# The scale and the sign of a softmax moved upstream, and two weight loads asked for earlier

## The chip, the cores and the metric

One core of a Trainium2 chip runs the whole program. The metric is the time of one execution on the device in microseconds (us); lower is better. The program before was timed three times; the median is compared. Engines are named as the profile does: PE is TensorE's matrix multiplication (PEld its weight loads, which overlap it), DVE is VectorE, ACT is ScalarE, POOL is GpSimd, SP is SyncE, which here only issues transfers.

## What is computed

Two layers of a decoder over 16 learned tokens and 1024 tokens, model width 1024. Layer 0 mixes with a recurrence and pooling, layer 1 with causal differential attention; after each mixer stand an output projection and an MLP. The change touches the attention of layer 1 and the beginning of what follows it. Of the reference:

```python
def one_block(args):
    qblk, start = args
    s = jnp.einsum('bqhcd,bkhcd->bhcqk', qblk, k).astype(jnp.float32) * scale
    qpos = start + jnp.arange(Q_BLOCK)
    mask = kpos[None, :] <= qpos[:, None]
    s = jnp.where(mask, s, -jnp.inf)
    p = jax.nn.softmax(s, axis=-1)
    attn = p[:, :, 0] - lam * p[:, :, 1]
    return jnp.einsum('bhqk,bkhe->bqhe', attn.astype(v.dtype), v)
...
for i in range(DEPTH):
    ...
    h = h + rmsnorm(m, g[1])
    f = sq_relu_mlp(rmsnorm(h, g[2]), mlp_w1[i], mlp_w2[i])
    h = h + rmsnorm(f, g[3])
```

Here q and k have 8 heads with two components c of 64 channels each, and scale is 1/8.

## The kernel before

All matrices are float32. A product of two of them is done as three products of halves: each operand is split into a rounded part "hi" (a copy on ACT) and the rest "lo" (a subtraction on DVE or POOL).

**The attention (mixer1)** goes over 8 heads, and in a head over 8 blocks of 128 queries (attn_block). The queries of a component are split in `halves` (L1756 on ACT, L1757 on DVE) into one operand qst that holds hi and lo; each key operand stands as kh and kl. In a block, for each component c, PE writes the scores s to a PSUM tile (L1824, L1826, and L1828 for the causal mask); there are two such tiles. DVE takes the row maximum into a column of m: where the block has up to 512 keys, one reduce for both components (L1834), above that one for each (L1831). The last block of a head has 1040 keys; the last 16 of both components stand in a tile se of their own and are folded in by L1836 and L1838. Then L1839 multiplies both columns of m by -1/8, and ACT forms exp(s/8 + m) with the row sum (L1843; L1845 for the 16 keys). L1850 and L1851 invert the sums, L1855 (ACT) and L1856 (DVE) combine the two components. The result is transposed on PE (L1870), split (L1873 on ACT, L1874 on DVE) and multiplied with the values (L1896 to L1903).

Beside this, work of the next head stands in the program: its weights are loaded to the one buffer R[0] with two halves (L360), split (L361 on ACT, L362 on POOL) and used in projections psq and psv (L377 to L379). In the last head, 7, there is no next head. There the first part of the output projection stands instead (`early`): loads of the earlier heads' outputs ho (L1533), their split (L397, L398), products pse (L377 to L379), a copy pz (L527) and its store to the DRAM tensor part (L528).

The order of mixer1 is not the text's. The framework schedules the instructions with its own estimates of their durations, so that an edit in one place can move rows on all engines. Each engine and each transfer queue then takes its row strictly in order.

**The late region (late)** ends the layer: the rest of the output projection (`tiles`), norms, and the MLP. For layer 1 it first needs five pieces of the output weights in split form: two narrow ones wl (128x640), which hold the last two row blocks for the five column blocks that `early` has begun, and three wide ones wo (128x1024). They are loaded to buffers raw (L669; R[0] takes the first two and the last, a second buffer the two between) and split into tiles opb (L670 on ACT, L671 on DVE). A product of `tiles` (L691) is 6 matmuls with wl or 24 with wo. What part holds is loaded to ac (L673, one load for each half of the tokens) and added (L721). The order here is set by the class Flow, a planner with costs of its own. The buffers of the late region lie where those of mixer1 were, and an instruction that first writes such a place waits for the last reader of what was there.

Of the kernel before, what the change touches and what calls it, by code (L numbers as in the profile page):

```python
# [7 lines left out]
F32 = mybir.dt.float32  # L8
F32R = mybir.dt.float32r
AF = mybir.ActivationFunctionType  # L10
ALU = mybir.AluOpType
# [4 lines left out]
T = 1040  # L16
NM = 16
# [46 lines left out]
LW = ((768, 768, 1024, 1024), (640, 640, 1024, 1024, 1024))  # L64
# [257 lines left out]
class Trunk:  # L322
# [231 lines left out]
    def late(self, l, xs, part, hin, hmid, hout, pre, rsb):  # L554

        nc, tc, A = self.nc, self.tc, self.A
# [32 lines left out]
        S = [rp.tile([P, NH], F32, name=f"ss{i}") for i in (0, 1)]  # L589
# [73 lines left out]
        for i in range(len(n)):  # L663
            hi, lo = self.lw(i)
            if True:
                z = ("R", i % 4 // 2, i % 2)
                raw = R[i % 4 // 2][:, i % 2, :n[i]]
                if l or i > 1:
                    F.dma(lambda raw=raw, i=i: nc.sync.dma_start(raw, self.lw_src(l, i)), n[i] * 512, w=[z])  # L669
                F.act(n[i], lambda raw=raw, hi=hi: nc.scalar.copy(hi, raw), r=[z], w=[("L", i, 0)])  # L670
                F.dve(n[i], lambda raw=raw, hi=hi, lo=lo: tt(lo, raw, hi.bitcast(F32), op=ALU.subtract), r=[z, ("L", i, 0)], w=[("L", i, 1)])  # L671
            if i < 2:
                F.dma(lambda h=i: nc.sync.dma_start(m[h][:, :ne], self.rows(part, off + NH * h, NH)), ne * P * 4 * NH, w=sum((nM(i, k) for k in range(ne)), []))  # L673
# [244 lines left out]
        for j in range(14):  # L918
# [7 lines left out]
            c = {11: 0, 21: 1, 22: 2, 12: 7}  # L926
# [49 lines left out]
        for b in range(4):  # L976
            nk = 4 if b < 3 else 2
            for q, i in enumerate(order):
                p = place[was[q]]
                st, z = H3[q % 2], nH(q % 2)  # L980
# [45 lines left out]
        for x in (0, 1):  # L1026
            st, z = H3[x], nH(x)
# [609 lines left out]
    def mixer1(self, hn):  # L1637
        tc, nc, A, dr = self.tc, self.nc, self.A, self.dr
        self.o1d = dr.tile([8, P, 1024], F32, name="o1d")
        part = dr.tile([5 * P, T], F32, name="part1")  # L1640
        lam_init = 0.8 - 0.6 * math.exp(-0.3)
        with tc.tile_pool(name="dps", bufs=2, space=PSUM, reuse_waits="tile") as dps, \
             tc.tile_pool(name="sps", bufs=2, space=PSUM, reuse_waits="tile") as sps, \
             tc.tile_pool(name="tps", bufs=1, space=PSUM, reuse_waits="tile") as tps, \
             tc.tile_pool(name="aps", bufs=1, space=PSUM, reuse_waits="tile") as aps, \
             tc.tile_pool(name="ep", bufs=1, reuse_waits="tile") as ep:
            self.dps, self.sps, self.tps, self.aps, self.ep = dps, sps, tps, aps, ep
            self.tp = ep
            self.cs = ep.tile([P, 2, T], F32, name="cs")
            nc.sync.dma_start(self.cs, A["rope"])  # L1650
            lv = ep.tile([P, 4, C], F32, name="lv")
            nc.sync.dma_start(lv, A["lamv"])
            self.identb = ep.tile([P, P], mybir.dt.bfloat16, name="identb")
            nc.vector.tensor_copy(self.identb, self.con[:, K_ID:K_ID + P])
            self.maskb = ep.tile([P, P], mybir.dt.bfloat16, name="maskb")
            cau = ep.tile([P, 512], F32, tag="sb", name="cau", bufs=4)[:, :P]
            nc.sync.dma_start(cau, A["con"][:, K_CAU:K_CAU + P])
            nc.vector.tensor_copy(self.maskb, cau)
            nc.vector.tensor_tensor(lv[:, 0:2], lv[:, 0::2], lv[:, 1::2], op=ALU.mult)
            l2 = ep.tile([P, 2], F32, name="l2")  # L1660
            nc.vector.tensor_reduce(l2, lv[:, 0:2], axis=mybir.AxisListType.X, op=ALU.add)
            nc.scalar.activation(l2, l2, AF.Exp)
            self.nlam = ep.tile([P, 1], F32, name="nlam")
            nc.vector.scalar_tensor_tensor(self.nlam, l2[:, 1:2], -lam_init, l2[:, 0:1], op0=ALU.add, op1=ALU.subtract)
            self.sub = ep.tile([P, 1], F32, name="sub")
            nc.vector.tensor_scalar(self.sub, self.par[:, C_SUB:C_SUB + 1], (lam_init - 1.0) * 0.5 / P, None, op0=ALU.mult)
            self.pt, self.ov = {}, {}
            wide = [w.rearrange("p a b -> p (a b)") for w in self.WP]
            self.ring, self.turn = [(wide[0], wide[1]), (wide[2], ep.tile([P, 1024], F32R, name="wpx"))], 0
            self.given = [((wide[0], wide[1]),), (None,)]  # L1670
            self.quarters = QS[1]
            xs = [[] for _ in QS[1]]
            early = self.early(xs, A["wo_1"], part, 6, 5)
            load = lambda k: [0 for _ in self.loads(xs, self.o1d, (k,), NM, 2)]
            fill = [lambda k=k: load(k) for k in range(6)] + [lambda: next(early)] * (4 * 5)
            fill.insert(max(len(fill) - 9, 6), lambda: load(6))
            qkv, first = self.attn_in(0, hn)
            for i in [0, 5, 1, 6, 10, 11, 2, 7, 3, 4, 12, 8, 9, 13, 14, 15]:
                first[i]()
            for b in (0, 1):  # L1680
                self.pt[0, b] = self.attn_block(0, b, qkv)
            for h in range(8):
                nxt, side = self.attn_in(h + 1, hn) if h < 7 else (None, fill[:30])
                main = self.attn(h, qkv, nxt)
                at = (0, 6, 12, 12, 14, 15, 16, 24, 24, 24, 24, 24, 24, 24, 29, 29) if h < 7 else [0 + i * 2 for i in range(len(side))]
                i = 0
                for n, f in enumerate(main):
                    while i < len(side) and at[i] <= n:
                        side[i]()
                        i += 1  # L1690
                    f()
                for f in side[i:]:
                    f()
                qkv = nxt
            for f in fill[30:]:
                f()
            for c in range(4):
                xs[c].append(self.x7[c])
            self.late_x = xs
        return part  # L1700

    def attn_in(self, h, hn):
        nc, ep, cs = self.nc, self.ep, self.cs
# [47 lines left out]
        def halves(nme):  # L1751
            for c in (0, 1):
                d = tl[nme, c]
                if nme == "q":
                    st = ep.tile([P, 1024], F32R, tag="qst", name=self.nm("qst"), bufs=2)
                    nc.scalar.copy(st, d[:, :1024])  # L1756
                    nc.vector.tensor_tensor(st[64:128], d[64:128, :1024], st[64:128].bitcast(F32), op=ALU.subtract)  # L1757
                    res["q", c] = st
                else:
                    kh = ep.tile([P, T], F32R, tag="kh", name=self.nm("kh"), bufs=2)  # L1760
                    kl = ep.tile([P, T], F32R, tag="kl", name=self.nm("kl"), bufs=2)
                    nc.scalar.copy(kh, d)
                    for a, b, e in ((0, 640, nc.vector), (640, T, nc.gpsimd)):
                        e.tensor_tensor(kl[:, a:b], d[:, a:b], kh[:, a:b].bitcast(F32), op=ALU.subtract)
                    res["k", c] = (kh, kl)
# [36 lines left out]
    def attn_block(self, h, i, qkv):  # L1802
        nc, ep = self.nc, self.ep
# [6 lines left out]
        for c in (0, 1):  # L1810
# [17 lines left out]
                    nc.tensor.matmul(out(x0, x1), self.identb, self.maskb[:, x0 - m0:x1 - m0], start=False, stop=True)  # L1828
            S.append(sp)
            if L > 512:  # L1830
                nc.vector.tensor_reduce(m2[:, c:c + 1], sp[:, :L0], axis=mybir.AxisListType.X, op=ALU.max)  # L1831
        if L <= 512:
            s3 = S[0].rearrange("p (c k) -> p c k", c=2)[:, :, :L]
            nc.vector.tensor_reduce(m2[:, 0:2], s3, axis=mybir.AxisListType.X, op=ALU.max)  # L1834
        if se is not None:
            nc.vector.tensor_reduce(m2[:, 4:6], se[:, :2 * NM].rearrange("p (c k) -> p c k", c=2),  # L1836
                                    axis=mybir.AxisListType.X, op=ALU.max)
            nc.vector.tensor_tensor(m2[:, 0:2], m2[:, 0:2], m2[:, 4:6], op=ALU.max)  # L1838
        nc.vector.tensor_scalar(m2[:, 0:2], m2[:, 0:2], -0.125, None, op0=ALU.mult)  # L1839
        pr = []  # L1840
        for c in (0, 1):
            p = ep.tile([P, T], F32, tag=f"p{c}", name=self.nm("p"), bufs=1 if c else 3)
            nc.scalar.activation(p[:, :L0], S[c][:, :L0], AF.Exp, bias=m2[:, c:c + 1], scale=0.125, accum_out=m2[:, 2 + c:3 + c])  # L1843
            if se is not None:
                nc.scalar.activation(p[:, 1024:T], se[:, c * NM:(c + 1) * NM], AF.Exp, bias=m2[:, c:c + 1], scale=0.125,  # L1845
                                     accum_out=m2[:, 6 + c:7 + c])
            pr.append(p)
        if se is not None:
# [236 lines left out]
```

## Time and profile before

| | us |
|---|---|
| median of 3 runs | 2778.07 (2774.0 to 2783.71) |
| the profiled execution | 2771.01 |
| its span, first to last instruction | 2769.1 |
| PE busy | 2614.2 (94%) |
| DVE busy | 2032.5 (73%) |
| ACT busy | 1342.7 (48%) |
| POOL busy | 290.4 (10%) |
| mean granted TensorE clock | 0.974 |

The attention of layer 1 lies about between 1440 and 2024 us of the span, the late region of layer 1 from there to the end. A row of the timeline has the start in us, the duration, the engine and the line, what is written<-read, and in brackets how long the engine stood idle before it and whom it waited for. A row with xN merges N neighbours. A row of the waits view has the waiting engine and line, the one waited for, then total us, times, and the longest. The row of a line has its duration in ns as smallest/median/largest.

### The profile page before, as it was taken

To read this page: it belongs to the slowest core of one execution; us is meant where nothing else is said; L and a number is where in the kernel's file an instruction comes from. 1 tells how busy PE (TensorE), PEld (TensorE's weight loads), DVE (VectorE), ACT (ScalarE), POOL (GpSimd) and SP (SyncE) were. 2 spreads that over 40 slices of the span, in tenths; PEclk is the share of its full clock that TensorE was granted. 3 is DMA by queue.
4 is the path that set the end of the run, shared out by engine and by line. 5 is a ranking of instruction groups with operands and counts; after the bars stand their busy time and mean duration, and the time that the engine had idled before them with its cause. 6 is when DMAs were issued, how large, how long until landed. Compare 5 with 4: busy or idle time off the path is not lost.

```text
span 2769.1 us, 44824 instructions
## 1 busy us (share of the span) xinstructions
PE 2614.2 (94%) x16950; PEld 2381.9 (86%) x16950; DVE 2032.5 (73%) x3742; ACT 1342.7 (48%) x2779; POOL 290.4 (10%) x410
## 2 busy tenths in 40 slices
PE   7999998899999999999968999999889999999997
PEld 6899897899899999999956899898787788778877
DVE  5356876534977777888786887888648778778888
ACT  5456776544633334343344556555636333443342
POOL 0111334220000000000012222222000000000000
PEclk9999998899999999999988999999999999999998
DMA  4456777554324345443332222222243243543443
GB/s 152 172 183 187 244 220 222 179 162 150 142 101 170 137 164 193 169 153 132 107 112 73 59 77 68 62 67 62 77 159 137 103 167 150 194 172 137 152 160 122
DMA packets 198575, 391.27 MB, mean 141 GB/s; under 512 B 59984, under 2 KB 122328, under 8 KB 185944
## 3 DMA queue, kind: packets, MB, share of 16 engines
q1 hardware_dynamic: 171176, 348.24, 37.8%
q10 hardware_dynamic: 27184, 40.18, 4.0%
q8 instruction: 133, 2.18, 0.3%
q14 instruction: 82, 0.67, 0.1%
HBM read 240.06 MB, written 131.38 MB: 134 GB/s over the span
## 4 chain that ended last, share of the span: by engine, by line
PE 64%; DVE 10%; ACT 4%; issue 2%; DMA 2%; POOL 0%; DVEq 0%; SPq 0%; ACTq 0%; POOLq 0%
PE bank L691 44%; PE psq L377 2%; PE psq L378 2%; PE psq L379 2%; PE ps L292 1%; PE s L1824 1%; PE tr L1870 1%; PE s L1826 1%; PE xs L292 1%; ACT p L1843 1%; DVE ac L1072 1%; DVE ac L1073 1%; DVE opb L818 1%; PE av L1896 1%; DVE ac L1001 1%
## 5 line engine op out<-in xcount | busy, mean ns | idle before, releaser
L691 PE MATMUL bank<-opa,wp 128*128 128x260 f32 (+1 forms) x3296 | 658.9, 320 | 8.6 <-DVE wp L782 5.3
L691 PEld LDWEIGHTS bank<-opa,wp 128*128 128x128 f32 x3296 | 518.0, 189 | 60.1 <-DVE wp L782 6.8
L691 PE MATMUL bank<-opb,wp 128*128 128x260 f32 (+1 forms) x1150 | 348.4, 324 | 1.8 <-DVE ac L1001 1.8
L292 PE MATMUL ps<-opa,whi 128*128 128x346 f32 (+2 forms) x1008 | 268.3, 328 | 4.7 <-DVE ys L292 4.0
L691 PE MATMUL bank<-opa,hh 128*128 128x260 f32 (+1 forms) x1112 | 241.1, 321 | 8.0 <-DVE hh L782 5.3
L691 PEld LDWEIGHTS bank<-opb,wp 128*128 128x128 f32 x1150 | 216.9, 189 | 21.0 <-ACT opa L1024 2.2
L1001 DVE TENSOR_TENSOR ac<-bank,ac 128x520 f32<-128x520 f32 (+1 forms) x256 | 171.6, 691 | 67.8 <-PE bank L691 66.5
L691 PE MATMUL bank<-opa,opb 128*128 128x260 f32 (+4 forms) x1168 | 206.1, 306 | 11.6 <-ACT opb L670 7.2
L691 PEld LDWEIGHTS bank<-opa,hh 128*128 128x128 f32 x1112 | 185.9, 191 | 24.4 <-DVE hh L782 5.8
L691 PEld LDWEIGHTS bank<-opa,opb 128*128 128x128 f32 x1168 | 168.2, 194 | 22.6 <-ACT opb L670 7.6
L292 PEld LDWEIGHTS ps<-opa,whi 128*128 128x128 f32 x1008 | 181.1, 192 | 6.5 <-DVE ys L292 4.8
L691 PE MATMUL bank<-opb,hh 128*128 128x260 f32 (+1 forms) x616 | 180.6, 327 | 0.0
L781 ACT CAST wp<-raw 128x512 fp32r<-128x512 f32 (+1 forms) x138 | 80.3, 584 | 184.6 <-PE bank L691 179.0
L292 PE MATMUL ps<-opa,wlo 128*128 128x346 f32 (+2 forms) x504 | 158.4, 314 | 0.0
L781 ACT CAST wp<-ss 128x512 fp32r<-128x512 f32 (+1 forms) x130 | 76.7, 590 | 164.5 <-PE bank L691 143.6
L1843 ACT ACTIVATE p<-s,m 128x272 f32<-128x272 f32 (+7 forms) x128 | 95.4, 750 | 85.4 <-DVE m L1839 83.6
L691 PE MATMUL bank<-opa,tt 128*128 128x260 f32 (+1 forms) x648 | 130.5, 318 | 0.2 <-DVE tt L782 0.2
L691 PEld LDWEIGHTS bank<-opb,hh 128*128 128x128 f32 x616 | 117.7, 191 | 9.9
L377 PE MATMUL psq<-opa,wp 128*128 128x346 f32 (+2 forms) x352 | 117.5, 334 | 4.4 <-DVE rp L462 2.6
L362 POOL TENSOR_TENSOR wpx<-raw,wp 128x1024 fp32r<-128x1024 f32 (+1 forms) x14 | 34.4, 2459 | 785.8 <-PE bank L691 742.8
L379 PE MATMUL psq<-opa,wp 128*128 128x346 f32 (+2 forms) x352 | 113.4, 322 | 0.0
L691 PE MATMUL bank<-opb,opb 128*128 128x256 f32 (+4 forms) x456 | 111.3, 308 | 0.5 <-DVE tt L747 0.5
(408 smaller groups left out, 6561.9 us busy)
## 6 DMA issues: line engine op xcount, KB each, us to landing
raw<-in_w_dram SPq DMA_DIRECT2D x64, 1024.0 KB
hid<-ac SPq DMA_DIRECT2D x14, 1820.0 KB
hid<-ac SPq DMA_DIRECT2D x14, 1792.0 KB
hh<-hid SPq DMA_DIRECT2D x23, 1040.0 KB
hh<-hid SPq DMA_DIRECT2D x23, 1024.0 KB
pk<-sg ACTq DMA_DIRECT2D x32, 704.0 KB
lt<-pk SPq DMA_DIRECT2D x32, 704.0 KB
raw<-in_w_qkv_dram SPq DMA_DIRECT2D x24, 512.0 KB
```

The lines of the kernel that those rows point to most:

```text
L292: one = eng, cost, lambda: fn(*args, **kw), r, w
L362: (lo or nc.gpsimd).tensor_tensor(lw[:, :n], raw[:, :n], hi[:, :n].bitcast(F32), op=ALU.subtract)
L377: nc.tensor.matmul(ps, wh, xh, start=(first and i == 0), stop=False)
L378: nc.tensor.matmul(ps, wl, xh, start=False, stop=False)
L379: nc.tensor.matmul(ps, wh, xl, start=False, stop=(last and i == n - 1))
L691: nc.tensor.matmul(ps, use(x), use(y), start=start and i == j == 0, stop=i == len(ws) - 1 and j == 2, skip_group_check=not start)
L781: F.act(n, lambda: nc.scalar.copy(use(t[0][:, :n]), src), r=rd, w=[z[0]] + claim)
L818: F.dve(4 * NH, lambda: tt(lo, use(src), hi.bitcast(F32), op=ALU.subtract), r=rd + wh, w=wl)
L1001: F.dve(NH, lambda d=d, q=q: tt(sv(d), q, sv(d), op=ALU.add), r=nq + nd, w=nd, ps=True)
L1072: F.dve(W, lambda d=d, k=k: stt(d, d, self.gcol(l, 3, k), y, op0=ALU.mult, op1=ALU.mult), r=nd + [ny], w=nd)
L1073: F.dve(W, lambda d=d, k=k: tt(d, d, use(H3[k // 4][:, k % 4, :W]), op=ALU.add), r=nd + [("H", k // 4, k % 4)], w=nd)
L1843: nc.scalar.activation(p[:, :L0], S[c][:, :L0], AF.Exp, bias=m2[:, c:c + 1], scale=0.125, accum_out=m2[:, 2 + c:3 + c])
```

## The change

The queries are multiplied by 1/8 when they are split. The reduces give the negated maximum, so that L1839 goes, and the fold of the 16 last keys takes the smaller value. The exponentials no longer scale. In the late region of layer 1 the loads of the two wl pieces are left out of the planner's list, and two loads of the same data to the same buffer stand at the end of mixer1 instead. (Layer 0 had this already.)

```diff
-                if l or i > 1:
+                if i > 1:
                     F.dma(lambda raw=raw, i=i: nc.sync.dma_start(raw, self.lw_src(l, i)), n[i] * 512, w=[z])
...
             for f in fill[30:]:
                 f()
+            self.lw_n = LW[1]
+            for i in (0, 1):
+                nc.sync.dma_start(self.R[0][:, i, :self.lw_n[i]], self.lw_src(1, i))
...
-                    nc.scalar.copy(st, d[:, :1024])
-                    nc.vector.tensor_tensor(st[64:128], d[64:128, :1024], st[64:128].bitcast(F32), op=ALU.subtract)
+                    nc.scalar.activation(st, d[:, :1024], AF.Copy, scale=0.125)
+                    nc.vector.scalar_tensor_tensor(st[64:128], d[64:128, :1024], 0.125, st[64:128].bitcast(F32), op0=ALU.mult, op1=ALU.subtract)
...
             if L > 512:
-                nc.vector.tensor_reduce(m2[:, c:c + 1], sp[:, :L0], axis=mybir.AxisListType.X, op=ALU.max)
+                nc.vector.tensor_reduce(m2[:, c:c + 1], sp[:, :L0], axis=mybir.AxisListType.X, op=ALU.max, negate=True)
         if L <= 512:
             s3 = S[0].rearrange("p (c k) -> p c k", c=2)[:, :, :L]
-            nc.vector.tensor_reduce(m2[:, 0:2], s3, axis=mybir.AxisListType.X, op=ALU.max)
+            nc.vector.tensor_reduce(m2[:, 0:2], s3, axis=mybir.AxisListType.X, op=ALU.max, negate=True)
         if se is not None:
             nc.vector.tensor_reduce(m2[:, 4:6], se[:, :2 * NM].rearrange("p (c k) -> p c k", c=2),
-                                    axis=mybir.AxisListType.X, op=ALU.max)
-            nc.vector.tensor_tensor(m2[:, 0:2], m2[:, 0:2], m2[:, 4:6], op=ALU.max)
-        nc.vector.tensor_scalar(m2[:, 0:2], m2[:, 0:2], -0.125, None, op0=ALU.mult)
+                                    axis=mybir.AxisListType.X, op=ALU.max, negate=True)
+            nc.vector.tensor_tensor(m2[:, 0:2], m2[:, 0:2], m2[:, 4:6], op=ALU.min)
...
-            nc.scalar.activation(p[:, :L0], S[c][:, :L0], AF.Exp, bias=m2[:, c:c + 1], scale=0.125, accum_out=m2[:, 2 + c:3 + c])
+            nc.scalar.activation(p[:, :L0], S[c][:, :L0], AF.Exp, bias=m2[:, c:c + 1], accum_out=m2[:, 2 + c:3 + c])
             if se is not None:
-                nc.scalar.activation(p[:, 1024:T], se[:, c * NM:(c + 1) * NM], AF.Exp, bias=m2[:, c:c + 1], scale=0.125,
+                nc.scalar.activation(p[:, 1024:T], se[:, c * NM:(c + 1) * NM], AF.Exp, bias=m2[:, c:c + 1],
```

The rows move at many places of the attention; three follow. Lines from L1699 on stand two or three higher in the changed program (L1843 is L1845 there). The first place is ACT's row in head 0, blocks 3 (528 keys) and 4 (656). An ACTIVATE that reads s is an exponential, component 0 first and then 1; p<-p is L1855, ah and axh are splits of transposed results, wp a weight split. Before:

```order
L1883 CAST axh_14160<-trx_14158 16x128
L1843 ACTIVATE p_14208,m_14190<-s_14191,m_14190 128x528
L1843 ACTIVATE p_14210,m_14190<-s_14199,m_14190 128x528
L1855 ACTIVATE p_14208<-p_14208,m_14190 128x528
L361 CAST wp_6334<-raw_743 128x1024
L1873 CAST ah_14254<-tr_14249 128x512
L1843 ACTIVATE p_14289,m_14273<-s_14274,m_14273 128x656
L1843 ACTIVATE p_14291,m_14273<-s_14281,m_14273 128x656
```

And now:

```order
L1845 ACTIVATE p_14204,m_14187<-s_14188,m_14187 128x528
L1885 CAST axh_14158<-trx_14156 16x128
L1845 ACTIVATE p_14206,m_14187<-s_14196,m_14187 128x528
L1857 ACTIVATE p_14204<-p_14204,m_14187 128x528
L1845 ACTIVATE p_14284,m_14269<-s_14270,m_14269 128x656
L361 CAST wp_6334<-raw_743 128x1024
L1875 CAST ah_14250<-tr_14245 128x512
L1845 ACTIVATE p_14286,m_14269<-s_14277,m_14269 128x656
```

The exponential of component 0 moved ahead of other work, away from that of component 1.

The second place is ACT's row in head 7, blocks 4 (656 keys) to 6 (912). opa<-ho is L397, the split of a loaded output of an earlier head. Before:

```order
L397 CAST opa_76<-ho_19333 128x256
L1873 CAST ah_19406<-tr_19401 128x512
L1843 ACTIVATE p_19473,m_19457<-s_19458,m_19457 128x656
L397 CAST opa_70<-ho_19382 128x256
L1843 ACTIVATE p_19475,m_19457<-s_19465,m_19457 128x656
L1873 CAST ah_19431<-tr_19426 128x512
L397 CAST opa_72<-ho_19386 128x256
L1855 ACTIVATE p_19473<-p_19473,m_19457 128x656
L397 CAST opa_74<-ho_19390 128x256
```

And now (the same loads have other numbers: ho_19275 was ho_19333, ho_19322 was ho_19382):

```order
L1845 ACTIVATE p_19412,m_19397<-s_19398,m_19397 128x656
L1875 CAST ah_19346<-tr_19341 128x512
L1845 ACTIVATE p_19414,m_19397<-s_19405,m_19397 128x656
L397 CAST opa_76<-ho_19275 128x256
L1875 CAST ah_19371<-tr_19366 128x512
L397 CAST opa_70<-ho_19322 128x256
L1845 ACTIVATE p_19436,m_19421<-s_19422,m_19421 128x784
L1885 CAST axh_19377<-trx_19375 16x128
L1857 ACTIVATE p_19412<-p_19412,m_19397 128x656
```

Both exponentials of block 4 moved ahead of a load's split that stood before them, and the first one of block 5 (784 keys) ahead of L1855 of block 4.

The third place is the start of the late region of layer 1, first the row of SP's transfers. raw_743 is R[0], raw the second buffer. Before:

```order
L669 DMA raw_743<-in_wl_dram 128x640
L669 DMA raw<-in_wo_dram 128x1024 x2
L673 DMA ac_20243<-part_13700 128x5x512
L669 DMA raw_743<-in_wl_dram 128x640
L755 DMA hh_20241<-h_68 128x4x512
L755 DMA hh_20242<-h_68 128x4x512
L673 DMA ac_20244<-part_13700 128x5x512
L669 DMA raw_743<-in_wo_dram 128x1024
```

And now:

```order
L1699 DMA raw_743<-in_wl_dram 128x640 x2
L669 DMA raw<-in_wo_dram 128x1024 x2
L673 DMA ac_20181<-part_13700 128x5x512
L755 DMA hh_20179<-h_68 128x4x512
L755 DMA hh_20180<-h_68 128x4x512
L669 DMA raw_743<-in_wo_dram 128x1024
L673 DMA ac_20182<-part_13700 128x5x512
```

The second wl load moved from behind the first load of part to the first place, and the third wo load ahead of the second load of part. DVE's row there, the splits (lo halves) and the first addition, before:

```order
L671 TENSOR_TENSOR opb_20222<-raw_743,opb_20222 128x640
L671 TENSOR_TENSOR opb_20224<-raw,opb_20223 128x1024
L671 TENSOR_TENSOR opb_20231<-raw,opb_20224 128x1024
L671 TENSOR_TENSOR opb_20223<-raw_743,opb_20222 128x640
L721 TENSOR_TENSOR ac_20243<-ac_20243,bank_20245 128x256
```

And now (opb_20160, 20161, 20162 and 20169 take the places of 20222, 20223, 20224 and 20231):

```order
L671 TENSOR_TENSOR opb_20160<-raw_743,opb_20160 128x640
L671 TENSOR_TENSOR opb_20161<-raw_743,opb_20160 128x640
L671 TENSOR_TENSOR opb_20162<-raw,opb_20161 128x1024
L671 TENSOR_TENSOR opb_20169<-raw,opb_20162 128x1024
L721 TENSOR_TENSOR ac_20181<-ac_20181,bank_20183 128x256
```

The second narrow split moved ahead of both wide ones. On PE the same happens: five products of 6 matmuls with wl, which stood behind two products of 24 with wo, now stand first; behind these seven products the rows of PE are the same as before.

## The prediction

> **What bounds the kernel now.** I read the stretches first (the windows view: busy time of each engine, then the TensorE clock granted), because the change touches two places only, the attention of layer 1 and the start of its late region.
>
> ```profile
> 1475.00:1545.00 70.00, 60.20 (x340) 50.36 (x339) 47.57 (x85) 36.46 (x73) 14.69 (x14) 0.88 0.25 68
> 1545.00:1925.00 380.00, 376.16 (x2454) 341.24 (x2455) 310.37 (x581) 222.66 (x448) 99.36 (x88) 1.00 0.24 66
> 1925.00:1975.00 50.00, 40.11 (x231) 31.99 (x231) 38.35 (x83) 33.93 (x82) 2.79 (x4) 0.90 0.22 71
> 1975.00:2024.00 49.00, 48.54 (x391) 46.17 (x390) 19.14 (x34) 22.95 (x52) 5.66 (x3) 1.00 0.30 92
> 2024.00:2035.00 11.00, 4.37 (x21) 3.88 (x21) 3.19 (x3) 3.19 (x4) 0.00 (x0) 0.69 1.02 379
> ```
>
> The columns are length, then PE, PEld, DVE, ACT and POOL, then clock. From 1545 to 1925 PE is busy 376.16 of 380 us at full clock: TensorE is the bound, and a shorter softmax buys next to nothing there. Three stretches are different. Head 0 (1475 to 1545) has 9.8 us without a matmul and a mean clock of 0.88, that is 70 x 0.12 = 8.4 us of clock withheld. Head 7 (1925 to 1975) has 9.9 us without a matmul and 5 us of withheld clock. At the change to the late region (2024 to 2035) PE works 4.37 of 11 us. Only there can time be had.
>
> In all three PE waits in a chain. The waits view, of the whole attention (1440 to 2010) and then of 1545 to 1925 alone, names the step that the change removes; the third row is its line:
>
> ```profile
> ACT p L1843 <- DVE m L1839: 83.6, 35, 8.6
> ...
> ACT p L1843 <- DVE m L1839: 70.5, 29, 4.7
> ...
> L1839 DVE TENSOR_SCALAR m<-m x64: 146/164/2272, 1484.1 to 1986.6; 128x2 f32<-128x2 f32 x64
> ```
>
> ScalarE's exponential (L1843) stood still 83.6 us for the small instruction that turns the maximum's sign (L1839, 64 of them, median 164 ns). But 70.5 us of that lie between 1545 and 1925, where ScalarE is busy 222.66 of 380 us and PE is full: that wait isn't a gain.
>
> **The change part by part. 1, the sign and the scale.** Sixty-four L1839 go: by the median 64 x 0.164 = 10.5 us of VectorE. The larger effect is that a join goes. L1839 took both columns of m, so that the exponential of component 0 waited for the maximum of component 1 too. Now each exponential waits for its own reduce. The timeline of head 0, blocks 0, 3 and 4, on VectorE and ScalarE:
>
> ```profile
> 1483.10 1.10 DVE L1834 TENSOR_REDUCE m<-s 128x2 f32<-128x288 f32 x2
> 1484.38 0.38 ACT L1843 ACTIVATE p<-s,m 128x144 f32<-128x144 f32 x1 [8.60 <-DVE m L1839]
> 1492.33 0.70 DVE L1831 TENSOR_REDUCE m<-s 128x1 f32<-128x528 f32 x1
> 1493.38 0.70 ACT L1843 ACTIVATE p<-s,m 128x528 f32<-128x528 f32 x1 [0.79 <-DVE m L1839]
> 1495.95 0.84 DVE L1831 TENSOR_REDUCE m<-s 128x1 f32<-128x656 f32 x1 [0.65 <-PE s L1828]
> 1497.39 0.83 DVE L1831 TENSOR_REDUCE m<-s 128x1 f32<-128x656 f32 x1
> 1498.26 1.45 DVE L1839 TENSOR_SCALAR m<-m 128x2 f32<-128x2 f32 x1
> 1499.74 0.81 ACT L1843 ACTIVATE p<-s,m 128x656 f32<-128x656 f32 x1 [0.69 <-DVE m L1839]
> ```
>
> Block 0: two reduces end at 1484.2 and the first exponential starts at 1484.38; the first reduce is over after half of the 1.10 us, so it can start some 0.6 us sooner. Block 4: component 0's reduce is over at 1496.8, its exponential starts at 1499.74, behind the second reduce and a stretched L1839 of 1.45 us. How much earlier a block gets is what stood between the first reduce and the sign: one reduce of component 1 and one L1839. The groups by shape give the reduces of blocks 3 to 6:
>
> ```profile
> L1831 DVE TENSOR_REDUCE m<-s 128x1 f32<-128x528 f32 x16 | 11.2, 699 | 0.3
> L1831 DVE TENSOR_REDUCE m<-s 128x1 f32<-128x656 f32 x16 | 13.4, 836 | 1.3 <-PE s L1828 0.6
> L1831 DVE TENSOR_REDUCE m<-s 128x1 f32<-128x784 f32 x16 | 15.4, 964 | 0.1
> L1831 DVE TENSOR_REDUCE m<-s 128x1 f32<-128x912 f32 x16 | 17.7, 1104 | 0.4 <-PE s L1828 0.4
> ```
>
> 0.70 + 0.84 + 0.96 + 1.10 = 3.6 us, with four L1839 4.25 us. Block 7 keeps its join (the 16 last keys of both components are folded in by one instruction), and blocks 0 to 2 have one reduce for both components. So **head 0** gets 4.25 + 0.6 (block 0) + 1.3 (the stretched L1839, 1.45 less a normal 0.15) = **6.1 us**, if all of it stands on the path. Bounds: nothing, where VectorE's own load binds (47.57 of 70 us); 18 us, if all idle time and withheld clock went. I take 6.1, a third of that.
>
> A rule of the skill bears on the 1.3 us. By the Trainium skill ("SBUF — State Buffer", "Who interferes with whom") a DVE tensor_scalar can lock the ports that it shares with GpSimd, and the later of the two waits out the other; a reduce never does. The trace agrees: GpSimd's L362 ran over the stretched one. By that rule the stall goes; if it only moved to the next VectorE instruction, head 0 would be 4.8 us.
>
> **Head 7** has the same four joins, 4.25 us, but ScalarE also waits there for loads of earlier heads' output (L1533 to L397):
>
> ```profile
> 1947.54 0.70 ACT L1843 ACTIVATE p<-s,m 128x528 f32<-128x528 f32 x1 [0.74 <-DVE m L1839]
> 1952.16 0.40 ACT L397 CAST opa<-ho 128x256 fp32r<-128x256 f32 x1 [1.88 <-DMA ho<-o1d]
> 1961.17 0.50 PE L1824 MATMUL s<-kh,qst 128*128 128x512 f32 x1 [1.89 <-ACT p L1843]
> 1966.64 0.41 ACT L397 CAST opa<-ho 128x256 fp32r<-128x256 f32 x1 [2.09 <-DMA ho<-o1d]
> 1945.63 25.47 SPq L1533 DMA_DIRECT2D ho<-o1d  x15
> ```
>
> Exponentials queued behind such a CAST waited 1.88 and 2.09 us for a transfer, and PE 1.89 us for an exponential. In the new order exponentials of the next block stand ahead of the CASTs, so the attention gets on while a load is under way. After 1975 PE is full (48.54 of 49), so what PE does sooner before 1975 comes off the end. Between 0 (the loads set the pace: fifteen in 25.47 us) and 9.9 us (all idle time), I take **4 us**, about the four joins.
>
> **In the middle heads** I count 0, covered by PE's 376 of 380 us; without that cover each of the six heads would gain up to the same 4.25 us.
>
> What is added is priced by neighbours. The queries' split changes its form on both engines:
>
> ```profile
> 2013.59 0.69 DVE L463 SCALAR_TENSOR_TENSOR sb<-sb,sb 128x512 f32<-128x512 f32 x1
> 2044.04 0.69 DVE L683 TENSOR_TENSOR ss<-ss,tt 128x512 f32<-128x512 f32 x1
> 2120.51 1.93 ACT L820 ACTIVATE opa<-hh 128x2048 fp32r<-128x2048 f32 x1
> 2129.27 1.91 ACT L817 CAST opa<-hh 128x2048 fp32r<-128x2048 f32 x1 [2.07 <-PE bank L733]
> ```
>
> The same length costs VectorE the same with a constant factor, and ScalarE 0.02 us more at 2048 elements: 16 + 16 instructions, 0.2 us at most, nothing on the path but two. No row has a reduce with turned sign. Between a gain of nothing (it reads the same elements) and the price of the separate pass that it replaces (0.164 us, which for 112 reduces would put 18 us back on VectorE), I take 0, as a sign needs no second pass over the data.
>
> **2, the raw weights.** The timeline at the end of the mixer, SP's queue, ScalarE and VectorE, and the row of the chain that starts PE again:
>
> ```profile
> 2006.67 0.33 SPq L669 DMA_DIRECT2D raw<-in_wl_dram  x1
> 2022.22 0.38 SPq L673 DMA_DIRECT2D ac<-part  x1
> 2022.65 0.52 SPq L669 DMA_DIRECT2D raw<-in_wl_dram  x1
> 2024.26 0.37 ACT L527 COPY pz<-pse 128x256 f32<-128x256 f32 x1 [1.74 <-PE pse L379]
> 2025.79 0.82 DVE L671 TENSOR_TENSOR opb<-raw,opb 128x640 fp32r<-128x640 f32 x1 [9.49 <-ACT opb L670]
> 2027.70 1.04 ACT L670 CAST opb<-raw 128x1024 fp32r<-128x1024 f32 x1 [1.94 <-DMA part<-pz]
> 2030.15 2.36 DVE L671 TENSOR_TENSOR opb<-raw,opb 128x1024 fp32r<-128x1024 f32 x2 [3.54 <-DMA part<-pz]
> 2031.43 31.23 PE bank L691 x251
> ```
>
> PE's last mixer product ended about 2024.2 and the next started at 2031.43. The second wl load sat behind the load of part (L673) on SP, from 2006.67 to 2022.65; therefore the order let the wide wo weights go first, and their low half (2030.15) waited for the last store of the mixer, whose buffer it overwrites. Now both wl loads are issued at about 2006.7, when GpSimd has read what stood in their buffer, and the two narrow splits come first. The second one's low half goes to the next tile of opb, which is free when the CAST of 2027.70 was. So it runs from 2027.7, 0.82 us, and PE starts at about 2028.6: **2.8 us** sooner. Five short products (30 matmuls at 31.23 / 251 = 0.124 us, 3.7 us) then cover the wide splits until 2032.3; the first wide low half is done by 2030.15 + 1.2 = 2031.35, in time. From there the order is that of before. SP is moved past as well: the third wo load now stands ahead of the second load of part, which waits for the same store as before; it needs the narrow split's end (2026.6), well ahead of that store. Bounds: 0, if the low half waits for both stores; 5, if neither.
>
> Beside the row of clock 0.69: the Trainium skill ("TensorE: Matmul & The Clock Gate", "Part 1: The HAM clock gate") says that the array falls to half clock after an idle window of about 3.4 us and returns after a busy one. The trace agrees, with no clock between. By that rule a shorter pause could spare a half-clock window (up to 1.7 us more) in each of the three places; I don't count it; it is the second rival below.
>
> Sum: 6.1 + 4 + 2.8 = 12.9 us. The profiled execution took 2771.01 us (span 2769.1 and 1.9 around it), 7 us under the median of 2778.07; off that execution the sum gives 2758.1, off the median, by which the result is judged, **2765**.
>
> **The rivals.** *Only the seam.* Head 0 is held by VectorE's load and head 7 by the loads of ho; each yields about 1 us, and with 2.8 us the time is 2773. For it: fifteen loads in 25.47 us, an almost closed chain; against it: VectorE idles 22 us in head 0. That an exponential still can't start early, since others stand ahead of it on ScalarE, ends here too.
> *The clock comes back.* With shorter pauses half of the 13.4 us of withheld clock in heads 0 and 7 goes on top of the sum: 2765 - 6.7 = 2758.
> *Slower: PE's queue blocks in the middle heads.* The new order puts scores earlier in PE's queue. PE takes instructions in order: a score product whose PSUM slot is not yet freed by an exponential stops projections behind it that could run. A wait was
>
> ```profile
> PE s L1824 <- ACT p L1843: 4.9, 6, 1.9
> ```
>
> 0.8 us on the mean. If 30 of the 48 middle blocks wait once, 24 us are lost against 12.9 won: 2789. It turns the result slower from about 26 such blocks on (12.9 + 8.3 us, over 0.8). Against it: in 380 us hardly a wait shows now, and exponentials come earlier, not later.
>
> **How the numbers follow.** A measurement can tell about 0.3%, 8.3 us, so faster means under 2769.7. Forecast 0.52 (0.44 faster, 0.08 same, as its terms may come out at two thirds), clock 0.14 (faster), seam 0.25 (0.06 faster, 0.19 same), slower 0.09 (0.08 slower, 0.01 same). That is 0.64, 0.28 and 0.08. The range 2754 to 2780 leaves out most of the slower case and the edges of the two others.
>
> **What would show it.** Right: no wait of L1843 on a second reduce; ScalarE's first exponential of block 4 of head 0 right behind its own reduce; PE's first late product 4.5 us after its last mixer product, not 7.2; clock above 0.88 and 0.90 in the head 0 and head 7 stretches. Wrong: scores waiting for exponentials in the middle heads, reduces longer than 0.70 to 1.10 us, or the attention's end at the same time with CASTs of ho waiting longer than 2 us.

## The result, and the profile after

The change made the kernel slower: 2808.93 us (median of 6 runs) against 2780.57 (median of 6 runs of the kernel before), ratio 1.0106 with a 95% interval of 1.0088 to 1.0123. The prediction was 2765, with a range of 2754 to 2780. The profiled execution's span went from 2769.1 to 2805.4 us. That is 36.3 us, where the medians differ by 28.4: the profiled execution of before (2771.01 us) was 9.6 us under its median, so the two traces show somewhat more of a loss than the medians. First the windows view of after, the two stretches of the prediction's first fence where the question lies (length, then PE, PEld, DVE, ACT, POOL, then the clock):

```profile
1475.00:1545.00 70.00, 62.82 (x350) 52.95 (x348) 47.24 (x82) 37.46 (x80) 14.46 (x14) 0.85 0.25 68
1545.00:1925.00 380.00, 357.75 (x2212) 320.70 (x2211) 280.59 (x481) 204.80 (x406) 84.21 (x78) 0.96 0.21 57
```

Head 0 did gain: PE works 62.8 of 70 us where it worked 60.2. But the middle stretch, where PE had been busy 376.16 of 380 us at full clock, now has 22 us without a matmul and 4% of its clock withheld. The whole attention, from the first score of head 0 to the last product with the values, in the same view of before and then of after:

```profile
1475.90:2007.30 531.40, 507.86 (x3277) 453.38 (x3276) 411.65 (x774) 309.51 (x640) 121.94 (x108) 0.97 0.24 67
```

```profile
1475.60:2045.50 569.90, 529.77 (x3277) 469.73 (x3276) 408.64 (x710) 313.25 (x640) 117.99 (x108) 0.94 0.22 63
```

It has the same 3277 matmuls and takes 38.5 us more: 16.6 us more without a matmul (40.1 instead of 23.5), and 21.9 us more in which the same matmuls run, about 18 of them as withheld clock (6% of 569.9 instead of 3% of 531.4). PE's waits from 1545 to 1925 in after show two large ones, each once in a head:

```profile
PE psv L377 <- DVE ab L1737: 10.5, 5, 2.1
PE s L1827 <- DVE qst L1760: 9.0, 5, 1.8
PE tr L1872 <- DVE p L1858: 2.3, 6, 0.7
```

Before, the same view of the same stretch held one such wait a head, for another row:

```profile
PE pst L1785 <- DVE vl L1788: 3.7, 5, 0.8
```

The timeline of one head in after, PE first (with the same row a head later), then POOL and DVE:

```profile
1592.36 0.43 PE L377 MATMUL psv<-opa,wp 128*128 128x346 f32 x1 [2.12 <-DVE ab L1737]
1606.59 0.30 PE L1827 MATMUL s<-kh,qst 128*128 128x144 f32 x1 [1.80 <-DVE qst L1760]
1664.89 0.43 PE L377 MATMUL psv<-opa,wp 128*128 128x346 f32 x1 [2.09 <-DVE ab L1737]
...
1588.26 2.96 POOL L362 TENSOR_TENSOR wpx<-raw,wp 128x1024 fp32r<-128x1024 f32 x1
1603.00 2.36 POOL L362 TENSOR_TENSOR wp<-raw,wp 128x1024 fp32r<-128x1024 f32 x1 [9.81 <-ACT wp L361]
...
1585.98 3.00 DVE L1767 TENSOR_TENSOR kl<-qkd,kh 128x640 fp32r<-128x640 f32 x2
1589.11 0.52 DVE L1735 TENSOR_TENSOR rp<-psq,cs 64x346 f32<-64x346 f32 x1
1589.66 1.57 DVE L1841 TENSOR_TENSOR m<-m 128x2 f32<-128x2 f32 x1
1591.79 0.52 DVE L1737 TENSOR_TENSOR ab<-psq,cs 128x346 f32<-128x346 f32 x1
1603.91 2.53 DVE L1760 SCALAR_TENSOR_TENSOR qst<-qkd,qst 64x1024 fp32r<-64x1024 f32 x1 [1.58 <-ACT qst L1759]
```

Read the **first stall** backwards. PE cannot start the second third of the values' projection (psv) until a PSUM bank is free. That bank holds the last third of the next head's queries (psq), and it is read out by the rotation, L1735 to L1737. The rotation stands behind the split of the keys (kl, 3.00 us), and in its middle stands L1841, two elements wide, which took 1.57 us and ended with POOL's L362 (1588.26 to 1591.22); that it waited for L362 is shown below ("The min as a reduce"). The **second stall**: the first scores of the next head need the low half of its queries, L1760, which took 2.53 us: it too ends 1.1 us after an L362 that ran over it (to 1605.36). One head is 1664.89 - 1592.36 = 72.5 us long (heads 1 to 6 take 70.5 to 73.8). The same places before, on PE (one row, and the same four heads later) and DVE:

```profile
1604.12 0.28 PE L1785 MATMUL pst<-con,vt 128*16 128x128 f32 x1 [0.76 <-DVE vl L1788]
1863.55 0.28 PE L1785 MATMUL pst<-con,vt 128*16 128x128 f32 x1 [0.75 <-DVE vl L1788]
...
1586.01 0.52 DVE L1732 TENSOR_TENSOR rp<-psq,cs 64x346 f32<-64x346 f32 x1 [1.25 <-PE psq L379]
1590.15 2.95 DVE L1764 TENSOR_TENSOR kl<-qkd,kh 128x640 fp32r<-128x640 f32 x2
1602.12 1.22 DVE L1757 TENSOR_TENSOR qst<-qkd,qst 64x1024 fp32r<-64x1024 f32 x1
```

There the rotation came as soon as psq was done, ahead of kl; the queries' low half took 1.22 us; a head was 259.43 / 4 = 64.9 us long. Why does kl stand ahead of the rotation now? The split of the keys writes buffers that the last block's scores of the head before still read. ACT's cast ahead of kl shows when they came free, in before and then in after:

```profile
1588.21 2.02 ACT L1762 CAST kh<-qkd 128x1040 fp32r<-128x1040 f32 x2 [0.22 <-PE se L1824]
```

```profile
1584.52 2.02 ACT L1765 CAST kh<-qkd 128x1040 fp32r<-128x1040 f32 x2 [0.99 <-PE se L1827]
```

With the join gone, exponentials come earlier, the scores of block 7 after them, and the keys' buffers are free 3.7 us sooner. The last product of psq ends at 1586 in both traces, so the keys' split used to be ready after the rotation and is now ready before it. The framework's scheduler takes what is ready first, and so puts the 3 us of kl where the rotation was. That it reasons so is inferred from the order; what the order costs was measured.

Behind both stalls the clock drops (windows view of after, the four pieces around them):

```profile
1590.20:1592.30 2.10, 0.04 (x1) 0.00 (x0) 2.06 (x4) 0.97 (x1) 1.15 (x2) 1.00 0.04 14
...
1593.70:1597.00 3.30, 3.30 (x14) 3.30 (x13) 1.72 (x4) 1.60 (x5) 0.00 (x0) 0.50 0.80 183
...
1604.70:1606.50 1.80, 0.09 (x1) 0.00 (x0) 1.77 (x2) 0.76 (x2) 0.65 (x1) 1.00 0.09 23
...
1607.20:1610.70 3.50, 3.50 (x18) 3.36 (x18) 2.04 (x4) 0.84 (x2) 0.00 (x0) 0.52 0.26 99
```

This head loses 2.1 + 1.8 us of stall and twice about 1.7 us of clock, 7.3 us. Less the 0.8 us that before lost to pst, that explains 6.5 of the 7.6 us by which it is longer. Not every stall has its half clock: over the stretch from 1545 to 1925 (380 us at a mean of 0.96, 5.2 heads) about 15 us are withheld, 2.9 a head.

### The profile page after: what moved, and what is told of

It reads as the page before. It is cut to its first block, busy times and chain, and to the rows that moved or that the text cites. A ratio compares the mean times of both kernels' runs of the same rounds, so it can differ in the third digit from the quotient of the medians.

```text
span 2805.4 us, 44742 instructions
## 1 busy us (share of the span) xinstructions
PE 2635.0 (94%) x16950; PEld 2396.6 (85%) x16950; DVE 2027.7 (72%) x3678; ACT 1346.1 (48%) x2779; POOL 286.9 (10%) x410
## 4 chain that ended last, share of the span: by engine, by line
PE 64%; DVE 11%; ACT 3%; issue 2%; DMA 2%; SPq 0%; POOL 0%; DVEq 0%; ACTq 0%; POOLq 0%
PE bank L691 43%; PE psq L377 2%; PE psq L378 2%; PE psq L379 2%; PE ps L292 1%; PE tr L1872 1%; PE s L1827 1%; PE s L1829 1%; PE xs L292 1%; DVE ac L1072 1%; PE psv L377 1%; PE psv L378 1%; PE psv L379 1%; DVE ac L1073 1%; DVE qst L1760 1%
## 5 line engine op out<-in xcount | busy, mean ns | idle before, releaser
L1001 DVE TENSOR_TENSOR ac<-bank,ac 128x520 f32<-128x520 f32 (+1 forms) x256 | 171.5, 691 | 68.3 <-PE bank L691 66.9
L1845 ACT ACTIVATE p<-s,m 128x272 f32<-128x272 f32 (+7 forms) x128 | 95.8, 750 | 50.1 <-DVE m L1841 22.4
L362 POOL TENSOR_TENSOR wpx<-raw,wp 128x1024 fp32r<-128x1024 f32 (+1 forms) x14 | 34.4, 2454 | 797.4 <-PE bank L691 740.7
```

Of the source, the lines that this page charges most:

```text
L362: (lo or nc.gpsimd).tensor_tensor(lw[:, :n], raw[:, :n], hi[:, :n].bitcast(F32), op=ALU.subtract)
L1001: F.dve(NH, lambda d=d, q=q: tt(sv(d), q, sv(d), op=ALU.add), r=nq + nd, w=nd, ps=True)
```

## The experiments

Ratios are to the kernel before on the same chip, with 95% intervals. The edits are shown shortened. The length of a head is counted in the timeline from one row to the same row of the next head.

**The loads alone.** The kernel before, with `if l or i > 1` made `if i > 1` and the new load loop.

> The kernel before with only the early loads of wl (softmax, scale and L1839 as before; the instructions of the attention keep their order on every engine). Theory (the loss comes from the order in which the attention's instructions now stand): the seam is worth what the change's trace shows, 2.1 us, so 2 us faster than before (ratio 0.999), attention heads 64.9 us apart as before. Rival (the early loads disturb the attention): 10 us slower or more.

Measured 2769.94 us, ratio 0.9985 (0.9975 to 0.9995); heads 64.9 us. The seam is a gain, and the loss isn't here.

**The scale alone.** The change, with plain reduces, `max`, and the join back:

```diff
-  ... op=ALU.max, negate=True)   (three reduces), op=ALU.min
+  ... op=ALU.max)                (three reduces), op=ALU.max
+  nc.vector.tensor_scalar(m2[:, 0:2], m2[:, 0:2], -1.0, None, op0=ALU.mult)
```

> The change with reduces of plain sign and L1839 put back (times -1), so that only the scale of the queries has moved; the attention's instructions stand in the order of before on every engine. Theory (order): as the loads alone, ratio 0.999, 2 us faster, the split of the queries (qst) at 1.22 us throughout. Rival (the new form of that split on VectorE is slow, 2.53 us, and makes the first scores of each head wait): 5 to 7 heads times 2.0 us and a half-clock window of 1.7 us behind each, 20 us or more slower.

Measured 0.9991 (0.9977 to 1.0004), heads 64.9 us. The row of the split of the queries in this run, with smallest/median/largest in ns:

```profile
L1760 DVE SCALAR_TENSOR_TENSOR qst<-qkd,qst x16: 1221/1222/1717, 1478.1 to 1937.6; 64x1024 fp32r<-64x1024 f32 x16
```

The new form isn't slow by itself; in after it is slow where it stands.

**The rotation first.** The change, with an edge for the scheduler only (no wait on the chip):

```diff
   r = nc.vector.tensor_tensor(ab[:, s], ps[:, off:W], cs[:, 0, s], op=ALU.mult)
+  if h and q and c == 2:
+      for x in (0, 1):
+          tc.add_manual_dep(kl_on_vector[x].ins, r.ins.name, NoSync)
```

> The change, with the split of the next head's keys (kl on VectorE) held behind the last rotation of its queries (the rope that frees a psq bank); only the order is fixed, nothing is computed differently. Theory (one displaced group on VectorE causes both stalls of a head): both go, heads 65 us apart instead of 72.5, and what head 0 and the seam gained is left: 2774, ratio 0.9976. If it causes only the first stall (2.2 us and 1.7 of half clock, 6 heads): 2786, ratio 1.002. Rival (the exponentials without the join crowd the middle heads in some other way): 2809, ratio 1.010.

Measured 0.9999 (0.9984 to 1.0013): nearly all of the loss is gone with one group of instructions put back. (The scheduler moved other rows with it, so this run shows that the order can be mended; what each stall costs is left to the runs that mend one at a time.) The first stall doesn't occur; of the second, 0.8 us a head stays:

```profile
PE s L1833 <- DVE qst L1764: 3.7, 5, 0.8
```

Heads are 66.9 us long, not 65, so the gains of head 0 and of the seam are used up. (The profiled execution, 2781.8 us, was 8.8 us above the run's median of 2773.0.)

**The rotation late, in the kernel before.** The reverse: the arithmetic of before, and the rotation held behind kl in the same way.

> The kernel before, arithmetic untouched, with the last rotation of the next head's queries held behind the split of its keys on VectorE, the order that the change came by. Theory: the stall of psv behind that rotation appears in heads 0 to 6 and with the half clock behind it costs at least 6 times 3.9 us: 2803 or more, ratio 1.008 or more. Rival (the order of these two does not matter, the removed join does): as before, ratio 1.000.

Measured 2831.25 us, ratio 1.0201 (1.0184 to 1.0218), heads 70 to 75 us. Its waits of PE from 1545 to 1925, and one row of its DVE:

```profile
PE psv L377 <- DVE ab L1737: 12.3, 5, 2.5
PE av L1901 <- ACT ah L1878: 9.0, 5, 1.8
PE s L1829 <- DVE qst L1760: 5.9, 5, 1.2
...
1684.84 2.54 DVE L1760 TENSOR_TENSOR qst<-qkd,qst 64x1024 fp32r<-64x1024 f32 x1 [1.56 <-ACT qst L1759]
```

An order of this kind makes both stalls, without any instruction of the change. But the run lost 56 us where the change lost 28: the edge moved more than the rotation, and a third wait came with it (av, 1.8 us a head) that the change doesn't have. So this run shows that the displaced rotation stalls psv, and not what the change's own order costs. The old form of the split, too, takes 2.54 us when it falls beside an L362 (1683.93 to 1686.29).

**The sign for each column.** The kernel before, with the join gone and nothing else of the change:

```diff
   if L > 512:
       nc.vector.tensor_reduce(m2[:, c:c + 1], sp[:, :L0], axis=X, op=ALU.max)
+      if se is None:
+          nc.vector.tensor_scalar(m2[:, c:c + 1], m2[:, c:c + 1], -0.125, None, op0=ALU.mult)
...
-  nc.vector.tensor_scalar(m2[:, 0:2], ...)
+  if L <= 512 or se is not None:
+      nc.vector.tensor_scalar(m2[:, 0:2], ...)
```

> The kernel before with nothing of the change but this: the sign and scale are applied to each column of m right behind its own reduce (blocks 3 to 6: two small instructions in place of one), so that the join is gone and no instruction is saved (96 small ones in place of 64). The order on VectorE puts the last rotation of the next head's queries behind the split of the keys, as the change does. Theory (the removed join moves the order, the order costs the time): heads about 72 us apart, ratio 1.010 to 1.014. Rival (something in the change's own instructions costs the time: negated reduces, min, scaled splits): no more than 1.001.

Measured 2817.67 us, ratio 1.0143 (1.0124 to 1.0161), heads 71 to 75 us, the same stall in front:

```profile
PE psv L377 <- DVE ab L1734: 12.2, 5, 2.5
PE s L1824 <- DVE qst L1757: 6.0, 5, 1.2
PE av L1899 <- ACT ah L1876: 5.3, 5, 1.1
```

So it is the join's removal that brings the displaced rotation, not the saved instructions, the negated reduces or the scale. The order isn't the change's row for row: here, too, av waits, 1.1 us a head.

**The join kept past head 0.** The change, plus `if h: nc.vector.tensor_scalar(m2[:, 0:2], m2[:, 0:2], 1.0, ...)`.

> The change, with a multiplication of both columns of m by 1.0 in heads 1 to 7, which puts the join back there; head 0 as in the change. The order of heads 1 to 7 is that of before. Theory (head 0 gains 4.3 us, the seam 2.1, middle heads nothing): 6.4 us faster than before, ratio 0.9977, heads 64.9 us apart, head 0 73.5. Rival (what head 0 gains is lost at the passage to head 1): as the loads alone, 0.9985 or above.

Measured 2771.39 us, ratio 0.9987 (0.9971 to 1.0002). The interval holds both expectations; the trace decides between them. The middle stretch is full again:

```profile
1545.00:1925.00 380.00, 376.09 (x2461) 341.64 (x2461) 311.02 (x578) 223.58 (x449) 101.55 (x89) 1.00 0.24 66
```

Head 0 is 73.5 us long instead of 78.1, head 1 68.3 instead of 65.9: 2.4 of the 4.6 us are given back at the passage, as the rival had it in part. All of the change's arithmetic is in this run, from early in head 1 on in the old order, and costs nothing that the trace shows.

**The min as a reduce.** The change, with L1841 alone in another form:

```diff
-  nc.vector.tensor_tensor(m2[:, 0:2], m2[:, 0:2], m2[:, 4:6], op=ALU.min)
+  nc.vector.tensor_reduce(m2[:, 8:10], m2[:, 0:8].rearrange("p (j c) -> p c j", c=4)[:, 0:2, :], axis=X, op=ALU.min)
```

> The change, with the min of block 7 (L1841, a tensor_tensor of 2 elements) written as a reduce of the same four numbers; every other instruction and the whole order are those of the change. Theory (L1841 sits out GpSimd's L362 because of its form, and the rotation behind it with it): 1.57 us become 0.17, the stall of psv shrinks from 2.2 to 0.8 us in 6 heads, 8 us; with the half clock behind it gone too, 18 us: ratio 1.0035 to 1.007. Rival (VectorE waits for GpSimd there whatever stands in the place): 1.010.

Measured 2787.04 us, ratio 1.0041 (1.0025 to 1.0057). POOL and DVE in this run, then its waits of PE from 1545 to 1925:

```profile
1659.05 2.97 POOL L362 TENSOR_TENSOR wp<-raw,wp 128x1024 fp32r<-128x1024 f32 x1
...
1660.46 0.16 DVE L1841 TENSOR_REDUCE m<-m 128x2 f32<-128x4 f32 x1
...
PE s L1827 <- DVE qst L1760: 9.0, 5, 1.8
PE psv L377 <- DVE ab L1737: 3.4, 5, 0.7
```

Apart from L1841 itself, every engine has the rows of the attention in the change's order. In the same place, under the same L362, the reduce takes 0.16 us. The first stall falls from 2.1 to 0.7 us, the second stays, and the ratio falls from the change's 1.0106 by 0.0065, 18 us of 2776: some 8 by the stall (1.4 us in six heads), the rest by the clock, whose mean over 1545 to 1925 is 1.00 in this run.

**The rotation's sum first, too.** As the rotation first, and on POOL its last sum ahead of the split of the keys, and the values' weights behind it.

> As the run with the rotation first, and on GpSimd too the sum that ends that rotation is held ahead of the split of the keys, and the split of the values' weights behind it, so that the queries' loads leave earlier. Theory (the second stall, the first scores of a head behind the split of the queries, comes from the late sum): it goes, heads 65 us apart, ratio 0.998. Rival (the second stall is only a meeting with GpSimd's L362): heads 66.9 apart as with the rotation first, ratio 1.000.

Both were wrong: ratio 1.0199 (1.0181 to 1.0216), heads 75 us.

```profile
PE psv L378 <- POOL wp L362: 16.5, 3, 5.6
PE psv L378 <- POOL wpx L362: 11.1, 2, 5.6
```

The low half of the values' weights now came 5.6 us late for psv. Whether an earlier sum alone would mend the second stall isn't answered by this run.

**The queries' split first.** The change, with `with tc.issue_after(first qst cast):` around the load and split of the next query weights, so that ACT's L361, and POOL's L362 behind it, come after the cast.

> The change, with the split of the query weights (L361 on ScalarE, and so L362 on GpSimd behind it) held behind the first cast of the queries to qst in each head; nothing is computed differently. Theory (the second stall of a head is qst's low half sitting out GpSimd's L362): L1760 takes 1.22 us instead of 2.53 there, the wait of the first scores falls from 2.0 to about 0.5 us and the half clock behind it goes; about 3.2 us in 6 or 7 heads, heads 69 us apart, ratio 1.0030 (1.002 to 1.005). Rival (the queries' loads land late, so that the scores wait all the same): 1.010.

Measured 2789.21 us, ratio 1.0049 (1.0037 to 1.0061), heads 68 us. L1760 (here L1763) takes 1.22 us throughout, now ahead of L362, and only the first stall is left (the scheduler also put one split of the values ahead of the queries' on ACT and DVE):

```profile
PE psv L377 <- DVE ab L1738: 10.5, 5, 2.1
...
PE s L1830 <- DVE qst L1763: 1.1, 5, 0.2
```

**Both mended.** The min as a reduce and the queries' split first, together.

> Both mendings together on the change: the min of block 7 as a reduce, and the split of the query weights held behind the first cast of the queries. Theory (the two stalls are the whole loss, each with its half clock): heads 65 to 66 us apart, 0.999 of before (0.997 to 1.001), with what head 0 and the seam gained kept. Rival (something else in the middle heads costs too): heads 67 us or more apart, ratio 1.003 or more.

Measured 2775.48 us, ratio 0.9999 (0.9989 to 1.0009):

```profile
1545.00:1925.00 380.00, 372.07 (x2396) 332.96 (x2396) 291.31 (x519) 220.74 (x435) 95.94 (x88) 1.00 0.22 64
```

Heads are 66.7 us long, between the two expectations. The two stalls, with their clock, are 5.8 of the 7.6 us. Of the other 1.8, PE's idle time explains 0.7 us a head (7.9 us of the 380 instead of 3.8, over 5.7 heads: what is left of the first stall, and transposes that wait for probabilities); 1.1 us stay unexplained. No version tried is measurably faster than the loads alone, which gain 0.15% on the kernel before.

## Why the prediction was wrong

**The step that failed** is the cover of the middle heads: "In the middle heads I count 0, covered by PE's 376 of 380 us". A busy PE covers what other engines do only as long as their order still feeds it. The order had changed, and what was late next was neither an exponential nor a score but a rotation that frees a PSUM bank, displaced by 3 us of kl. The price is 7.6 us in the head shown and 7.1 on the mean of heads 1 to 6, together about 43 us, where the sum had 0. Mending the two stalls ("Both mended") took the ratio from 1.0106 to 0.9999.

**The slower rival** had the right place (PE's queue blocked in order, in the middle heads), with the wrong cause and too small a size: it put thirty waits of 0.8 us on exponentials, and its 2789 is 11 us above before, where 28 were measured. There were two waits a head, of 1.8 and 2.1 us, on DVE rows, and the clock nearly doubled them. Its chance of 0.09 leaned on "hardly a wait shows now", which is a property of the old order.

**Head 0** was forecast at 6.1 us and gave 4.6 (78.1 to 73.5). The mechanism is as told: block 4's first exponential starts right behind its own reduce, which keeps its time.

```profile
1495.93 0.84 DVE L1834 TENSOR_REDUCE m<-s 128x1 f32<-128x656 f32 x1 [2.08 <-PE s L1831]
...
1496.80 0.81 ACT L1845 ACTIVATE p<-s,m 128x656 f32<-128x656 f32 x1 [2.44 <-DVE m L1834]
```

But the clock in that stretch fell to 0.85 instead of rising above 0.88, so "the clock comes back" was wrong too. Up to 1535.6 the mean is 0.86 over 60.6 us, 8.5 us withheld, as before; the rest is a half-clock stretch behind a stall of 1.1 us at the passage to head 1, where PE waits for that head's qst.

**Head 7** was forecast at 4 us and gave none: from its first score to the last product with the values it takes 78.7 us before and 79.7 after. The low bound was the right one, the loads of ho set the pace (fourteen in 26.82 us), and PE waited for a CAST of ho:

```profile
1983.06 26.82 SPq L1533 DMA_DIRECT2D ho<-o1d  x14
...
2002.67 0.38 PE L377 MATMUL pse<-opa,wp 128*128 128x256 f32 x1 [2.37 <-ACT opa L397]
```

**The seam** was forecast at 2.8 us; counted to the end of the 252nd late product it gave 2.1 (36.3 us behind the last mixer product instead of 38.4), and the loads alone 4.2 of 2775 us, with an interval of 1.4 to 6.9. The prediction overlooked a product of before: PE's first late product came at 2028.80 and not at 2031.43, and its next only then. The row of before, then two of after:

```profile
2028.80 0.58 PE L691 MATMUL bank<-opa,opb 128*128 128x256 f32 x1 [4.57 <-ACT opb L670]
...
2063.93 0.38 PE L691 MATMUL bank<-opa,opb 128*128 128x256 f32 x1 [1.58 <-ACT opb L670]
...
2067.20 12.98 PE L691 MATMUL bank<-opa,opb 128*128 128x256 f32 x91 [1.40 <-DVE opb L671]
```

The order is as told. The first product starts 1.6 us after the last of the mixer instead of 4.6; the run without a stop starts at 2067.20, 4.9 us behind it where 4.5 were forecast, after one more stop, at half clock.

**The forms of the instructions** cost nothing, as forecast: the negated reduces keep their time (128x656: 0.84 us in both), and the split of the queries takes 1.22 us where it stands free. The rule of the Trainium skill that the prediction weighed ("SBUF — State Buffer", "Who interferes with whom") was used too narrowly. The same section says that a DVE instruction with two SBUF inputs contends with a GpSimd instruction that reads SBUF. The trace agrees: L1841 (1.57 us against 0.16 as a reduce) and the split of the queries (2.53 against 1.22) are such, and L1735, which reads PSUM and SBUF, keeps its 0.52 us under the same L362. That rule, put beside the new order, would have priced the stretched part of each stall, 1.4 and 1.3 us, but not the place of kl ahead of the rotation. Part of kl's 3.00 us may be such a meeting as well: L671, a subtraction of the same shape, takes 0.82 us, so two would be 1.6 (an estimate), and POOL's half of the same split runs beside it (1585.65 to 1588.29). That wasn't tried.

## What to carry to other kernels

A wait that costs nothing can still hold an order together: where a scheduler sets the order, ask of a removed wait not only who was waiting but what now becomes ready earlier, and what that is put ahead of on the same engine. On an engine with slack, look for the few rows that free a buffer of the bound engine; displaced by 3 us they stop it, however idle the rest is. And a row's duration in the old trace may not hold in its new place: beside a GpSimd instruction of 3 us, a DVE row of 0.14 us took 1.57 here.

## What the runs showed of the hardware

The clock's drop didn't follow from the length of a pause alone. In after, the half-clock stretches last 3.41 us or a multiple and begin at whole multiples of it from each other (1593.7 and 1607.4, four apart), and a pause of 1.80 us was followed by one. In the same trace a pause of 2.12 us (to 1737.73) was followed by none: the clock stayed at 1.00 from 1737.8 to 1750.4. In the run with the queries' split first, pauses of 2.09 to 2.12 us were followed by none, and the clock stayed at 1.00 over the stretch that holds five of them:

```profile
1596.47 0.43 PE L377 MATMUL psv<-opa,wp 128*128 128x346 f32 x1 [2.12 <-DVE ab L1738]
...
1545.00:1925.00 380.00, 365.67 (x2354) 325.80 (x2353) 292.11 (x511) 215.31 (x431) 89.40 (x84) 1.00 0.22 61
```

Most of the numbers fit a count over fixed windows of 3.41 us: the pause of 1.80 us lay whole within one window, while those five, and the one to 1737.73, were each shared by two, with 1.3 to 1.7 us in the larger part. Not all fit: a pause of 1.79 us to 1822.83 was shared too, 1.4 us of it ahead of 1822.40, and the clock was 0.50 from there to 1829.2. So what the window counts stays open; it wasn't tried by itself. The Trainium skill ("TensorE: Matmul & The Clock Gate", "Part 1: The HAM clock gate") says that the window runs freely, which agrees; it speaks of an idle window of about 3.4 us, and here a window with 1.8 us of pause was enough. The trace agrees with the prediction's reading that there is no clock between 0.5 and 1, not with a threshold of a whole window. So a pause of 2 us cost 2 us, or 3.7 with a half-clock stretch behind it. In the min's run the second stall, unmended, lost most of its half clocks as well; that its pauses fell otherwise into the windows is the likely reason, and luck.
